# Attention of a two-layer hybrid decoder on one core: four heads a step in row quarters, rotary on another engine, keys ahead of values

## The chip, the cores and the metric

One core of a Trainium2 chip runs the whole program: two layers of a decoder for one sequence of 256 positions, in float32. The metric is the device time of one execution in microseconds. Engines are named as the profile names them: PE is TensorE (PEld its weight loads), DVE is VectorE, ACT is ScalarE, POOL is GpSimd, SP is SyncE, whose queue issues all DMAs here.

## The reference, cut to what matters

Each layer projects the normed input with one matrix, whose columns belong to a gated DeltaNet branch (16 heads of 128), a sliding-window attention branch (32 query heads of 64, 4 key/value heads, window 128) and two output gates:

```python
h   = rmsnorm(x, norm_w) * (1.0 + scale) + shift      # adaLN: shift, scale, gate from c
u   = h @ w_in
qkv_a, beta_a, a_a, z_a, q_b, k_b, v_b, z_b, g_a, g_b = split_cols(u, SPLIT_SIZES)
qkv_a = silu(causal_conv(qkv_a, conv_w))              # then l2norm of q_a and k_a per head
beta, g = sigmoid(beta_a), -exp(a_log) * softplus(a_a + dt_bias)
o_a = rmsnorm(gated_delta_rule(q_a, k_a, v_a, g, beta), gdn_norm_w) * silu(z_a)
q_b, k_b = rope(q_b, positions), rope(k_b, positions) # [x1 cos - x2 sin, x2 cos + x1 sin], halves of 32
o_b = swa_with_sinks(q_b, k_b, v_b, sinks) * silu(z_b)
y   = sigmoid(g_a) * (o_a @ proj_a) + sigmoid(g_b) * (o_b @ proj_b)
x   = x + gate * (y @ w_out)
```

The delta rule works in chunks: it forms decayed Gram products of the keys, solves a unit lower triangular system, and passes one state per head on. Attention scores have a causal window of 128, a learned sink logit per head in the softmax's denominator, and two blocks of 128 queries, the second of which sees the first block's keys too.

## The kernel before, in words

Activations lie transposed, channels on partitions and the 256 positions along the free dimension. The unit of work is one projection: a tile of 128 output columns of a weight matrix, contracted over 16 blocks of 128 channels. Weights come in halves of 128x1024 by DMA (`load_half`, lines 198 to 205); ACT rounds each to a high part (`whi`, L203) and DVE subtracts to get the low part (`wlo`, L204), so that float32 accuracy comes from matmuls in the rounded type: 16 of 512 columns with the high weights (L291) and 16 of 256 with the low ones (L292). There are five buffers for a loaded half, four for the high and three for the low part, and two PSUM banks (`psm`) for projections. `evac` (L317 to L320) takes a projection out of PSUM: ACT copies one half, DVE adds the other (L319). So the projection after next needs DVE's sum.

`_plan` (L46) lists a layer's projections in order; the gates of layer 0 and eight of layer 1 are done ahead in other code. Then follow `ba` (decay and beta), `kb` and `vb` (attention keys and values of two key/value heads each), and for each of two batches of eight DeltaNet heads: eight queries `qa`, eight values `va`, eight keys `ka`, and eight pairs of `qb` and `zb` (attention queries and their gate, two heads each). In the second batch the second `kb` and `vb` stand between values and keys. After both batches come `za` (the DeltaNet gate), and the three output matrices `pa`, `pb`, `wo`.

Each projection has a handler (`h_qa`, `h_zb`, ...), which runs as the code is written out. A handler may be a generator: `yield n` puts what follows behind n further projections beside the next one (`streams`, `advance`). One further generator per batch, `gdn`, is the delta rule; `run_bg(1)` writes out one of its steps after each projection. It is appended when the batch's last pair of keys has been handled. Its parts: decay and key norms (`E`, `GT`, L603, L615), Gram products (L623 to L626), a triangular solve of 32-row blocks as a chain of 62 DVE operations (L643 to L651), block products on PE (L673 to L705), and `gdn_core` with the state and the outputs. `ADA_RATE` says how many conditioning jobs (`ada_job`: two DMAs of 512 KB and two DVE operations, L170) go with each projection.

What is written out is not the order in which an engine works. The tile layer orders each engine's instructions ahead of time: an instruction written earlier goes first, unless by the layer's own durations its operands are not there yet; then later ones pass it. In the trace the product of L634, written late in `gdn_k`, runs in the value stage. On the chip each engine keeps that order and waits where an operand comes later.

An attention pair: `rope` (L793) shifts 32-row quarters with four DMAs and makes three POOL operations (L798, L799, L801); the scores (L836) contract the 64 rows of one head, the two heads of a pair in the two halves of the array's rows; DVE reduces them (L843, L845), ACT takes exponentials and scales, PE transposes (L864), ACT copies, PE multiplies by the values (L872, L873), DVE multiplies by the gate, and a DMA stores. Small PSUM tiles come from a ring of six banks (`psg`).

## Time and profile before

| what | value |
| --- | --- |
| median of 3 runs | 2387.16 us (2384.02 to 2390.58) |
| profiled execution | 2388.38 us, span 2386.6 us, granted TensorE clock 0.991 |
| PE busy | 2306.3 us, 97% |
| PEld busy | 2024.4 us, 85% |
| DVE busy | 1793.7 us, 75% |
| ACT busy | 1426.7 us, 60% |
| POOL busy | 120.3 us, 5% |
| DMA | 222 GB/s of HBM traffic over the span |
| chain that ended last | PE 70%, DVE 14%, DMA 9%, issue 3%, ACT 3%, POOL 1% |

The span is the time from the first to the last instruction. Busy time is the union of an engine's instructions; matmuls are pipelined, so a busy PE is not PE at its peak, and an idle PE is a real loss. The chain is followed back from the last instruction, at each step to what released it. By the order of projections in the trace, layer 0 has its DeltaNet and attention stages from 218 to 942 us and layer 1 from 1273 to 1968 us; layer 0 also carries most of the conditioning jobs.

### The profile page before, as it was taken

To read this page: it belongs to the slowest core of one execution; us is meant where nothing else is said; L and a number is where in the kernel's file an instruction comes from. 1 tells how busy PE (TensorE), PEld (TensorE's weight loads), DVE (VectorE), ACT (ScalarE), POOL (GpSimd) and SP (SyncE) were. 2 spreads that over 40 slices of the span, in tenths; PEclk is the share of its full clock that TensorE was granted. 3 is DMA by queue.
4 is the path that set the end of the run, shared out by engine and by line. 5 is a ranking of instruction groups with operands and counts; after the bars stand their busy time and mean duration, and the time that the engine had idled before them with its cause. 6 is when DMAs were issued, how large, how long until landed. Compare 5 with 4: busy or idle time off the path is not lost.

```text
span 2386.6 us, 40186 instructions
## 1 busy us (share of the span) xinstructions
PE 2306.3 (97%) x14838; PEld 2024.4 (85%) x14838; DVE 1793.7 (75%) x3117; ACT 1426.7 (60%) x2676; POOL 120.3 (5%) x128
## 2 busy tenths in 40 slices
PE   7999999999999999999999999999999999999997
PEld 6999787878878888888888888888888888888886
DVE  7998878877787868888676777856678457677766
ACT  4436656777657755444455667777677665444442
POOL 0000000120002100000000001100011000000000
PEclk9999999999999999999999999999999999999999
DMA  9998667566776567998756555555555557777764
GB/s 364 361 360 280 227 223 246 157 192 200 229 234 196 175 220 263 329 308 304 226 191 205 177 179 171 163 181 163 190 170 163 172 179 269 241 247 245 245 202 144
DMA packets 192519, 536.50 MB, mean 225 GB/s; under 512 B 42753, under 2 KB 76609, under 8 KB 186817
## 3 DMA queue, kind: packets, MB, share of 16 engines
q1 hardware_dynamic: 192322, 533.93, 67.1%
q8 instruction: 117, 1.92, 0.3%
q14 instruction: 80, 0.66, 0.1%
HBM read 512.26 MB, written 16.88 MB: 222 GB/s over the span
## 4 chain that ended last, share of the span: by engine, by line
PE 70%; DVE 14%; DMA 9%; issue 3%; ACT 3%; POOL 1%; SPq 0%; DVEq 0%; ACTq 0%; POOLq 0%
PE mm L291 35%; PE mm L292 18%; DVE wlo L204 5%; DMA adaw<-ada 3%; PE mmg L253 2%; PE mmg L251 2%; PE mmg L252 2%; DMA win<-w 2%; DMA xs_dram<-x 1%; DVE LX L649 1%; DMA rr<-rr_d 1%; DVE mt L647 1%; DVE cv L526 1%; ACT whi L203 1%; PE sc L836 1%
## 5 line engine op out<-in xcount | busy, mean ns | idle before, releaser
L291 PE MATMUL mm<-h,whi 128*128 128x512 f32 x3616 | 1298.0, 399 | 15.3 <-DVE ub L319 15.0
L204 DVE TENSOR_TENSOR wlo<-win,whi 128x1024 fp32r<-128x1024 f32 x724 | 886.2, 1227 | 302.6 <-PE mm L292 181.2
L292 PE MATMUL mm<-h,wlo 128*128 128x256 f32 x3616 | 1028.9, 285 | 0.0
L203 ACT CAST whi<-win 128x1024 fp32r<-128x1024 f32 x724 | 755.0, 1048 | 418.5 <-PE mm L291 237.7
L291 PEld LDWEIGHTS mm<-h,whi 128*128 128x128 f32 x3616 | 684.1, 189 | 172.4 <-issue 8.7
L292 PEld LDWEIGHTS mm<-h,wlo 128*128 128x128 f32 x3616 | 684.9, 189 | 1.4 <-issue 0.6
L170 DVE SCALAR_TENSOR_TENSOR adaw<-adaw,cact 128x1024 f32<-128x1024 f32 x128 | 156.0, 1225 | 58.6 <-DMA adaw<-ada 58.4
L291 PE MATMUL mm<-yhl,whi 128*128 128x512 f32 x512 | 181.1, 396 | 5.0 <-DVE x L926 3.4
L291 PE MATMUL mm<-oAhl,whi 128*128 128x512 f32 x512 | 180.8, 395 | 0.3 <-ACT whi L203 0.3
L291 PE MATMUL mm<-oBhl,whi 128*128 128x512 f32 x512 | 180.7, 396 | 0.0
L319 DVE TENSOR_TENSOR ub<-ub,mm 128x256 f32<-128x256 f32 x290 | 120.5, 415 | 60.5 <-ACT ub L318 60.4
L526 DVE SCALAR_TENSOR_TENSOR cv<-ub,par,cv 128x253 f32<-128x253 f32 (+2 forms) x288 | 137.7, 480 | 34.8 <-ACT cv L524 31.0
L292 PE MATMUL mm<-oAhl,wlo 128*128 128x256 f32 x512 | 144.3, 282 | 1.4 <-DVE wlo L204 1.4
L251 PE MATMUL mmg<-h,whi 128*128 128x256 f32 x512 | 139.5, 287 | 6.3 <-ACT h L376 6.1
L292 PE MATMUL mm<-yhl,wlo 128*128 128x256 f32 x512 | 144.4, 282 | 0.0
L292 PE MATMUL mm<-oBhl,wlo 128*128 128x256 f32 x512 | 144.1, 281 | 0.0
L252 PE MATMUL mmg<-h,whi 128*128 128x256 f32 x512 | 142.5, 286 | 0.1
L253 PE MATMUL mmg<-h,wlo 128*128 128x256 f32 x512 | 135.5, 287 | 3.2 <-DVE wlo L204 3.2
L318 ACT COPY ub<-mm 128x256 f32<-128x256 f32 x290 | 106.7, 368 | 47.0 <-PE mm L292 45.0
L291 PEld LDWEIGHTS mm<-yhl,whi 128*128 128x128 f32 x512 | 96.2, 188 | 29.5 <-issue 5.5
L291 PEld LDWEIGHTS mm<-oAhl,whi 128*128 128x128 f32 x512 | 96.1, 188 | 23.2 <-ACT whi L203 0.6
L291 PEld LDWEIGHTS mm<-oBhl,whi 128*128 128x128 f32 x512 | 96.2, 188 | 22.9
(260 smaller groups left out, 2764.3 us busy)
## 6 DMA issues: line engine op xcount, KB each, us to landing
win<-w SPq DMA_DIRECT2D x724, 512.0 KB, 4.9
adaw<-ada SPq DMA_DIRECT2D x128, 512.0 KB, 5.0
adab<-ada SPq DMA_DIRECT2D x31, 1024.0 KB, 8.9
sg<-sig_dram SPq DMA_DIRECT2D x40, 128.0 KB, 3.0
rot<-ub SPq DMA_DIRECT2D x144, 32.0 KB, 3.0
sig_dram<-gacc SPq DMA_DIRECT2D x4, 1024.0 KB
E<-gc_dram SPq DMA_DIRECT2D x4, 1024.0 KB
GT<-GT_d SPq DMA_DIRECT2D x4, 1024.0 KB
```

What stands on the lines that cost most here:

```text
L170: V.scalar_tensor_tensor(t, t, 1.0, cact[:, hf * 1024:(hf + 1) * 1024], op0=ALU.mult, op1=ALU.mult, accum_out=acc[:, hf:hf + 1])
L203: A.copy(h, w)
L204: V.tensor_tensor(o, w, h.bitcast(F32), op=ALU.subtract)
L251: T.matmul(d, hi, m[:, 0:S], start=(k == b0 and t % 2 == 0), stop=False)
L252: T.matmul(d, hi, m[:, S:2 * S], start=False, stop=False)
L253: T.matmul(d, lo, m[:, 0:S], start=False, stop=(k == b1 - 1 and t % 2 == 1))
L291: T.matmul(ps[:, :], hi[k // 8][:, c0:c0 + P], m, start=(k == 0), stop=False)
L292: T.matmul(ps[:, S:2 * S], lo[k // 8][:, c0:c0 + P], m[:, 0:S], start=False, stop=(k == KT - 1))
L318: A.copy(t, ps[:, S:2 * S])
L319: V.tensor_tensor(t, t, ps[:, 0:S], op=ALU.add)
L526: V.scalar_tensor_tensor(y[:, j:], u[:, :S - j], w(3 - j), y[:, j:], op0=ALU.mult, op1=ALU.add)
L647: V.tensor_tensor(tv, Xt[:, 0:j + 1, j:j + 1].broadcast_to([64, j + 1, n]), Lt[:, j:j + 1, j + 1:32].broadcast_to([64, j + 1, n]), op=ALU. ...
```

## The change

The plan puts both `kb` and both `vb` first, keys ahead of values in each batch, and attention as eight steps of four projections per layer: two of queries, two of gates. A query tile now holds one rotary half (32 channels) of four heads, one head of each key/value group, in the four 32-row quarters; the next tile holds the other halves. Key tiles are packed in the same way. Rotary then needs no shift: six DVE operations on whole tiles (`rope`), where four DMAs and three POOL operations stood for each tile. The sign column of the sine table goes.

A step (`h_zb`, every second gate) has four heads: scores as two accumulated products of 32 rows in one row quarter per head, four score banks; the softmax over four heads at once; transposes three projections later instead of two, copied back in place; values one projection after that, for two gate tiles; then both stores. The score matmuls are written right behind the second gate's projection.

The decay chain of `h_ba` is cut in three by yields. Pair transposes of `qa`, `ka` and `va` (`sumsq`, L723) are written after two further projections instead of one. One more background step stands before the block products of the solve. The conditioning rate of value projections falls from 0.35 to 0, that of attention projections rises from 0.1 to 0.275, in layer 0. The value tile of attention gets two buffers, `zbs` and the table scratch four.

```diff
-ADA_RATE = [dict(qa=0.45, ka=0.45, va=0.35, qb=0.1, zb=0.1, za=0.54, pa=0.54, pb=0.54), dict(ga=0.3, pa=0.3, gb=0.3, pb=0.3)]
+ADA_RATE = [dict(qa=0.45, ka=0.45, va=0.0, qb=0.275, zb=0.275, za=0.54, pa=0.54, pb=0.54), dict(ga=0.3, pa=0.3, gb=0.3, pb=0.3)]
...
-    p += [("ba", 0), ("kb", 0), ("vb", 0)]
+    p += [("ba", 0), ("kb", 0), ("kb", 1), ("vb", 0), ("vb", 1)]
     for b in range(NB):
-        for what in ("qa", "va", "ka"):
+        for what in ("qa", "ka", "va"):
             p += [(what, b * HB + h) for h in range(HB)]
-            if b == 1 and what == "va":
-                p += [("kb", 1), ("vb", 1)]
-        for t in range(8 * b, 8 * b + 8):
-            p += [("qb", t), ("zb", t)]
+        for j in range(4 * b, 4 * b + 4):
+            p += [("qb", 2 * j), ("qb", 2 * j + 1), ("zb", j), ("zb", 8 + j)]
...
-    if what == "qb":
-        return OFF_QB + _pair_rows(i)
+    if what in ("qb", "kb"):
+        heads = (i // 2 + 8 * np.arange(4)) if what == "qb" else np.arange(4)
+        return {"qb": OFF_QB, "kb": OFF_KB}[what] + (64 * heads[:, None] + 32 * (i % 2) + np.arange(32)).reshape(-1)
...
+            sink4 = sm.tile([P, 8, 4, 2], F32, name="sink4", tag="sink4", bufs=1)
...
             def h_ba(ps, i):
                 u = evac(ps)
+                yield 0
...
                 V.tensor_tensor(q, q, na.unsqueeze(1).broadcast_to([P, 2, NH]), op=ALU.mult)
+                yield 1
                 pg = gps("gcp", [P, 3, NH])
...
                 A.activation(egc1, gc[:, 1, :], AF.Exp)
+                yield 0
                 s = cols_to_rows(gc.rearrange("p m h -> p (m h)"), 2 * NH, "gcr")
...
                 conv_silu(ps, i, g["qT"][:, hh, :])
                 if hh % 2 == 1:
-                    yield 0
+                    yield 1
                     sumsq(g["qT"], g["ssq"], hh - 1)
...
                 conv_silu(ps, 16 + i, g["kT"][:, hh, :])
                 if hh % 2 == 1:
-                    yield 0
+                    yield 1
                     sumsq(g["kT"], g["ssk"], hh - 1, g["kdec"])
...
                         dma(d, xdr[:, blk].rearrange("q j i -> j q i"))
                 yield 1
                 yield 1
+                yield 1
                 GTv = GT.rearrange("p h m t -> p (h m) t")
...
                 pair = (g["vT"], vT)
-                yield 0
+                yield 1
                 p = gps("vtr", [P, 2, 2, P])
...
-            def rope(u, dst_pairs):
-                rot = sm.tile([P, S], F32, name="rot", tag="tB", bufs=2)
-                for a in range(4):
-                    c = a ^ 1
-                    dma(rot[32 * a:32 * a + 32, :], u[32 * c:32 * c + 32, :])
-                G.tensor_tensor(rot, rot, stab, op=ALU.mult)
-                G.tensor_tensor(u, u, ctab, op=ALU.mult)
-                for rows, dst in dst_pairs:
-                    G.tensor_tensor(dst, u[rows], rot[rows], op=ALU.add)
+            def rope(lo, hi, dst):
+                a = sm.tile([P, S], F32, name="rot", tag="tB", bufs=2)
+                V.tensor_tensor(a, hi, stab, op=ALU.mult)
+                b = sm.tile([P, S], F32, name="rot", tag="tB", bufs=2)
+                V.tensor_tensor(b, lo, stab, op=ALU.mult)
+                V.tensor_tensor(lo, lo, ctab, op=ALU.mult)
+                V.tensor_tensor(dst[:, 0, :], lo, a, op=ALU.subtract)
+                V.tensor_tensor(hi, hi, ctab, op=ALU.mult)
+                V.tensor_tensor(dst[:, 1, :], hi, b, op=ALU.add)
+
+            def halves(ps, i, name):
+                u = evac(ps)
+                if i % 2 == 0:
+                    st["lo"] = u
+                    return
+                r = sm.tile([P, 2, S], F32, name=name, tag=name, bufs=1)
+                rope(st["lo"], u, r)
+                st[name] = r
 
             def h_kb(ps, i):
-                u = evac(ps)
-                kp = sm.tile([P, S], F32, name="kr", tag="kr", bufs=1)
-                rope(u, [(slice(0, 128), kp)])
-                kpad[i] = kp
+                halves(ps, i, "kr")
...
-                v = sm.tile([P, 2, P], F32, name="vnat", tag="vnat", bufs=1)
+                v = sm.tile([P, 2, P], F32, name="vnat", tag="vnat", bufs=2)
...
-            def h_qb(ps, t):
-                u = evac(ps)
-                q = sm.tile([P, S], F32, name="qr", tag="tC", bufs=1)
-                rope(u, [(slice(0, 128), q)])
-                st["q"] = q
+            def h_qb(ps, i):
+                halves(ps, i, "qr")
 
             def h_zb(ps, t):
                 z = evac(ps)
-                zs = sm.tile([P, S], F32, name="zbs", tag="tD", bufs=3)
+                zs = sm.tile([P, S], F32, name="zbs", tag="tD", bufs=4)
                 A.activation(zs, z, AF.Silu)
-                q = st["q"]
-                yield 0
-                j = t // 8
-                kp, vn = kpad[j], vnat[j]
-                sc = [gps("sc", [P, 3 * P]) for _ in range(2)]
-                for e, m in ((0, 0), (1, 1), (0, 1), (1, 0)):
-                    r = slice(64 * e, 64 * e + 64)
-                    T.matmul(sc[e][:, m * P:(2 * m + 1) * P], q[r, m * P:(m + 1) * P], kp[r, 0:(m + 1) * P],
-                             start=True, stop=True)
-                pb = sm.tile([P, 2, 3 * P], F32, name="pb", tag="pb", bufs=1)
-                nm = sm.tile([P, 2, 2], F32, name="nm", tag="nm")
-                ls = sm.tile([P, 2, 2], F32, name="ls", tag="ls")
-                for e in range(2):
-                    ns = nsink[:, 2 * t + e:2 * t + e + 1]
+                if t < 8:
+                    st["z"] = zs
+                    return
+                j = t - 8
+                gates = (st["z"], zs)
+                q, k = st["qr"], st["kr"]
+                sc = [gps("sc", [P, 3 * P]) for _ in range(4)]
+                for m in range(2):
+                    for c in range(2):
+                        for e in range(4):
+                            r = slice(32 * e, 32 * e + 32)
+                            T.matmul(sc[e][:, m * P:(2 * m + 1) * P], q[r, c, m * P:(m + 1) * P],
+                                     k[r, c, 0:(m + 1) * P], start=(c == 0), stop=(c == 1))
+                pb = sm.tile([P, 4, 3 * P], F32, name="pb", tag="pb", bufs=1)
+                nm = sm.tile([P, 4, 2], F32, name="nm", tag="nm")
+                ls = sm.tile([P, 4, 2], F32, name="ls", tag="ls")
+                for e in range(4):
+                    ns = nsink[:, 4 * j + e:4 * j + e + 1]
                     V.tensor_tensor_reduce(pb[:, e, 0:P], sc[e][:, 0:P], amask[:, P:2 * P], -0.125, ns,
                                            ALU.add, ALU.min, nm[:, e, 0:1])
                     V.tensor_tensor_reduce(pb[:, e, P:3 * P], sc[e][:, P:3 * P], amask, -0.125, ns,
                                            ALU.add, ALU.min, nm[:, e, 1:2])
-                for e in range(2):
+                for e in range(4):
                     A.activation(pb[:, e, 0:P], pb[:, e, 0:P], AF.Exp, bias=nm[:, e, 0:1], scale=-1.0,
                                  accum_out=ls[:, e, 0:1])
                     A.activation(pb[:, e, P:3 * P], pb[:, e, P:3 * P], AF.Exp, bias=nm[:, e, 1:2], scale=-1.0,
                                  accum_out=ls[:, e, 1:2])
-                V.tensor_tensor(nm, nm, sink4[:, t], op=ALU.add)
+                V.tensor_tensor(nm, nm, sink4[:, j], op=ALU.add)
                 A.activation(nm, nm, AF.Exp)
                 V.tensor_tensor(ls, ls, nm, op=ALU.add)
                 V.reciprocal(ls, ls)
-                for e in range(2):
+                for e in range(4):
                     A.mul(pb[:, e, 0:P], pb[:, e, 0:P], ls[:, e, 0:1])
                     A.mul(pb[:, e, P:3 * P], pb[:, e, P:3 * P], ls[:, e, 1:2])
-                yield 1
+                yield 2
                 ptS = []
-                for e in range(2):
+                for e in range(4):
                     pt = gps("ptr", [P, 3, P])
                     for c in range(3):
                         T.transpose(pt[:, c, :], pb[:, e, c * P:(c + 1) * P], ident)
-                    ps_ = sm.tile([P, 3, P], F32, name="pts", tag="pts")
-                    A.copy(ps_, pt)
-                    ptS.append(ps_)
-                yield 1
-                po = gps("pv", [P, S])
-                for e in (1, 0):
-                    r = slice(64 * e, 64 * e + 64)
-                    T.matmul(po[r, :], vn[:, 0, r], ptS[e][:, 0:2, :], start=True, stop=False)
-                    T.matmul(po[r, P:S], vn[:, 1, r], ptS[e][:, 2, :], start=False, stop=True)
-                V.tensor_tensor(zs, zs, po, op=ALU.mult)
-                dma(ob_dram[t], zs)
+                    p = pb[:, e, :].rearrange("p (c q) -> p c q", c=3)
+                    A.copy(p, pt)
+                    ptS.append(p)
+                yield 0
+                for f in range(2):
+                    po = gps("pv", [P, S])
+                    vn = vnat[f]
+                    for e in (1, 0):
+                        r = slice(64 * e, 64 * e + 64)
+                        p = ptS[2 * f + e]
+                        T.matmul(po[r, :], vn[:, 0, r], p[:, 0:2, :], start=True, stop=False)
+                        T.matmul(po[r, P:S], vn[:, 1, r], p[:, 2, :], start=False, stop=True)
+                    V.tensor_tensor(gates[f], gates[f], po, op=ALU.mult)
+                    dma(ob_dram[8 * f + j], gates[f])
```

The rest moves the sink logits into the new order of heads.

## Rows read from the trace of the kernel before

**Rows 1.** Stretches: start:end, length; busy us of PE, PEld, DVE, ACT, POOL; clock; DMA.

```profile
2103.40:2283.20 179.80, 179.80 (x1026) 157.21 (x1025) 128.60 (x186) 86.73 (x127) 0.00 (x0) 1.00 0.73 240
291.10:342.40 51.30, 47.63 (x275) 40.95 (x274) 41.22 (x66) 29.65 (x61) 0.00 (x0) 1.00 0.70 235
```

**Rows 2.** PE's waits: who waited for whom: us in total, times, longest us.

```profile
PE mm L291 <- DVE ub L319: 15.0, 12, 2.6
PE sst L533 <- ACT kT L527: 8.5, 7, 3.0
PE vtr L723 <- ACT vT L527: 7.7, 6, 1.9
...
PE sc L836 <- POOL qr L801: 3.5, 4, 1.3
...
PE gcp L502 <- DVE spq L500: 3.2, 2, 1.8
```

**Rows 3.** Stretches: one attention pair, then the four that hold a solve.

```profile
446.14:460.04 13.90, 13.90 (x87) 11.68 (x87) 10.78 (x32) 11.52 (x25) 2.20 (x3) 1.00 0.59 190
...
447.00:493.00 46.00, 43.28 (x259) 36.20 (x258) 41.36 (x103) 34.55 (x72) 8.16 (x9) 0.96 0.61 195
765.00:805.00 40.00, 38.50 (x241) 32.22 (x240) 39.07 (x103) 29.30 (x59) 6.27 (x6) 1.00 0.53 169
1480.00:1534.00 54.00, 52.87 (x336) 44.53 (x335) 46.64 (x113) 39.46 (x78) 12.59 (x14) 1.00 0.52 164
1779.00:1832.00 53.00, 51.77 (x327) 43.50 (x327) 46.58 (x113) 38.48 (x78) 11.43 (x13) 1.00 0.53 161
```

**Rows 4.** PE in order of time, end of one pair: start us, us, instruction, count.

```profile
458.43 0.66 PE L872 MATMUL pv<-pts,vnat 128*64 128x256 f32 x4
...
459.24 0.87 PE L864 MATMUL ptr<-cst,pb 128*128 128x128 f32 x6
460.04 0.93 PE L836 MATMUL sc<-kr,qr 64*128 64x128 f32 x8
460.89 0.50 PE L291 MATMUL mm<-h,whi 128*128 128x512 f32 x1
```

**Rows 5.** PE groups by shape, first attention stage: count, busy us, mean ns, idle before.

```profile
L836 PE MATMUL sc<-kr,qr 64*128 64x256 f32 x32 | 7.2, 402 | 0.0
L836 PE MATMUL sc<-kr,qr 64*128 64x128 f32 x32 | 6.9, 297 | 2.5 <-POOL qr L801 2.5
```

**Rows 6.** DVE groups: whole kernel (first), layer 1's first attention stage (others).

```profile
L170 DVE SCALAR_TENSOR_TENSOR adaw<-adaw,cact 128x1024 f32<-128x1024 f32 x128 | 156.0, 1225 | 58.6 <-DMA adaw<-ada 58.4
...
L319 DVE TENSOR_TENSOR ub<-ub,mm 128x256 f32<-128x256 f32 x16 | 6.6, 411 | 4.1 <-ACT ub L318 4.1
L845 DVE CUSTOM_DVE_ANT_0 pb<-sc,cst,nsink 128x256 f32<-128x256 f32 x12 | 5.7, 475 | 0.0
L843 DVE CUSTOM_DVE_ANT_0 pb<-sc,cst,nsink 128x128 f32<-128x128 f32 x12 | 4.1, 342 | 1.8 <-PE sc L836 1.8
```

**Rows 7.** One line's and one tile's instructions: count: ns min/median/max, first and last start.

```profile
L204 DVE TENSOR_TENSOR wlo<-win,whi x724: 1161/1222/1809, 17.9 to 2365.3; 128x1024 fp32r<-128x1024 f32 x181
...
L647 DVE TENSOR_TENSOR mt<-LX x124: 183/368/958, 452.1 to 1837.0; 64x31 f32<-64x31 f32 x8, 64x60 f32<-64x60 f32 x8, 64x87 f32<-64x87 f32 x8, 64x112 f32<-64x112 f32 x8
L649 DVE TENSOR_TENSOR LX<-LX,mt x124: 182/357/976, 452.4 to 1837.2; 64x31 f32<-64x31 f32 x8, 64x60 f32<-64x60 f32 x8, 64x87 f32<-64x87 f32 x8, 64x112 f32<-64x112 f32 x8
```

**Rows 8.** DVE in order of time; POOL rotates from 466.86 to 469.56.

```profile
451.25 0.16 DVE L852 TENSOR_TENSOR nm<-nm,sink 128x4 f32<-128x4 f32 x1
...
465.63 0.39 DVE L649 TENSOR_TENSOR LX<-LX,mt 64x231 f32<-64x231 f32 x1
...
467.08 0.70 DVE L852 TENSOR_TENSOR nm<-nm,sink 128x4 f32<-128x4 f32 x1
...
468.13 0.83 DVE L649 TENSOR_TENSOR LX<-LX,mt 64x240 f32<-64x240 f32 x1
468.89 0.69 DVE L854 TENSOR_TENSOR ls<-ls,nm 128x4 f32<-128x4 f32 x1
```

More of the change, by code (lines that the diff above doesn't have):

```diff
@@ L87, in _tile_cols @@
         return c
-    if what == "qb":
-        return OFF_QB + _pair_rows(i)
+    if what in ("qb", "kb"):
+        heads = (i // 2 + 8 * np.arange(4)) if what == "qb" else np.arange(4)
+        return {"qb": OFF_QB, "kb": OFF_KB}[what] + (64 * heads[:, None] + 32 * (i % 2) + np.arange(32)).reshape(-1)
     if what == "zb":
         return OFF_ZB + _pair_rows(i)
-    off = {"ka": OFF_K, "va": OFF_V, "qa": OFF_Q, "kb": OFF_KB, "vb": OFF_VB,
+    off = {"ka": OFF_K, "va": OFF_V, "qa": OFF_Q, "vb": OFF_VB,
            "za": OFF_ZA, "ga": OFF_GA, "gb": OFF_GB}[what]
@@ L99 @@
 CC_ID, CC_TRI, CC_DM, CC_AM, CC_IF = 0, 128, 256, 384, 640
-NCC = 642
+NCC = 641
 def _consts():
@@ L115, in _consts @@
     c[:, CC_IF] = inv[i % half]
-    c[:, CC_IF + 1] = np.where((i % 64) < half, -1.0, 1.0)
     return c
@@ L338, in rope_tables @@
                 n = sm.tile([P, S], F32, name="nrot", tag="tC", bufs=1)
-                r = sm.tile([P, S], F32, name="rred", tag="tD", bufs=3)
+                r = sm.tile([P, S], F32, name="rred", tag="tD", bufs=4)
                 V.tensor_scalar(n, ang, 1.0 / (2.0 * math.pi), shift, op0=ALU.mult, op1=ALU.add)
@@ L441, in build @@
             edec = sm.tile([P, NH], F32, name="edec", tag="edec")
-            sink4 = sm.tile([P, 16, 2, 2], F32, name="sink4", tag="sink4", bufs=1)
-            V.tensor_copy(sink4, pr[:, PC_SINK:PC_SINK + 32].rearrange("p (t e) -> p t e", e=2).unsqueeze(3)
-                          .broadcast_to([P, 16, 2, 2]))
+            sink4 = sm.tile([P, 8, 4, 2], F32, name="sink4", tag="sink4", bufs=1)
+            V.tensor_copy(sink4, pr[:, PC_SINK:PC_SINK + 32].rearrange("p (t e) -> p t e", e=4).unsqueeze(3)
+                          .broadcast_to([P, 8, 4, 2]))
             nsink = sm.tile([P, 32], F32, name="nsink", tag="nsink", bufs=1)
@@ L449, in build @@
             yA = [None, None]
-            kpad, vnat = [None, None], [None, None]
+            vnat = [None, None]
             sig = {}
@@ L1051, in pack @@
     par = np.zeros((L, P, NPC), np.float32)
-    heads = np.concatenate([_pair_heads(t) for t in range(16)])
+    heads = np.concatenate([j + 8 * np.arange(4) for j in range(8)])
     for l in range(L):
```

1 line of the change is left out of this document (removed).

## The prediction

> **What bounds the kernel now.** I read the busy shares first, then the stages as stretches, then TensorE's own waits, then one attention pair instruction by instruction, and last VectorE. Where nothing else happens, 32 projections take 179.80 us, 5.62 us each, with TensorE busy throughout at a granted clock of 1.00 [rows 1]. That is the floor: a change can gain only what TensorE does or waits for between projections. The reader is to see that in the layer-0 value stage of the first batch the same eight projections, with their pair transposes, leave TensorE idle for 51.30 - 47.63 = 3.7 us [rows 1], and that the waits name the causes: transposes that wait for ScalarE's SiLU output (keys 8.5 us in 7 waits, values 7.7 us in 6), score matmuls that wait for GpSimd's rotary add (3.5 us in 4), and projections that wait for VectorE to empty a PSUM bank (15.0 us in 12) [rows 2].
>
> One undisturbed attention pair is 13.90 us from score block to score block [rows 3], so beside two projections (11.24) it costs 2.66. Its blocks start at 458.43 (values), 459.24 (transposes), 460.04 (scores), and the projections go on at 460.89 [rows 4]: 0.81, 0.80 and 0.85 us, and 0.2 more in the first projection matmul, which is longer than usual (0.50). What is work in it? The 256-column score matmul is 105 ns longer than the 128-column one (402 against 297) [rows 5], so 128 columns are 0.105 us. Per head a pair streams four score records of 128, 128, 256 and 256 columns, 768 in all, 0.63 us; both heads of the pair run at once, since eight records fit into 0.85 us. The value block has as many columns, 0.63. Six transposes are 6 x 0.105 = 0.63. So 1.89 us is work and 0.77 is four changes of the array's shape (projection to values, to transposes, to scores, to projection), 0.19 each.
>
> VectorE is the second limit. The triangular solve of the delta rule is a chain of 62 operations, and in the four stretches that hold it TensorE is idle by 46.00 - 43.28, 40.00 - 38.50, 54.00 - 52.87 and 53.00 - 51.77, together 6.6 us [rows 3].
>
> **The change, part by part.**
>
> *Later transposes.* Pair transposes of queries, keys and values are written one projection later than now, 5.6 us. The longest of the waits is 3.0 us for keys and 1.9 for values [rows 2], so the operand is there before its new place. Gain 8.5 + 7.7 = 16.2 us. What is late next is the square sums, which nobody needs for several projections. Bounds: 0 (if the order on the engines doesn't follow) to 16.2. I take all of it.
>
> *Rotary on VectorE.* Thirty-six rotations, each of four small copies in SyncE's queue and three GpSimd operations, become 18 of six VectorE operations. The scores were waiting for these; now two projections lie between the rotation and its scores. Gain 3.5 us [rows 2]. 144 DMA issues leave SyncE's queue; no TensorE wait of weight that I saw hangs on it, so nothing is taken for them.
>
> *Row quarters.* A step has four heads. Its scores contract 32 rows twice where a pair contracted 64 once: 2 x 768 columns per head, 1.26 us if the four quarters run at once. Values are 2 x 0.63, twelve transposes 1.26, and there are three changes of shape (projection to values to scores to projection; the transposes now stand between projections of their own shape): 3 x 0.19. Sum 4.35 against 2 x 2.66 = 5.32, 0.97 us for each of 16 steps, 15.5. I take 13, since some of the transposes' 0.80 may be a start that stays. The trace before shows only two row tiles at once, so the bounds come from it: four at once 1.26 us; two at once 2.52, which costs 20 us over all steps; one at a time 5.04, which costs 60. I take four, because the two that are shown do not delay each other at all: eight records with 1.26 us of columns take 0.85.
>
> The Trainium skill's "TensorE: Matmul & The Clock Gate" (Measured speedup vs the span model) gives 3.07 times for four row tiles, not 4. By it the scores of a step would be 5.04 / 3.07 = 1.64 us, an estimate, and the forecast 0.38 x 16 = 6 us higher, about 2374.
>
> *The solve under a heavier VectorE.* Keys ahead of values starts the delta rule's background work six projections earlier against the attention stage: its decay and Gram products fall into the value stage, and the solve into the first attention step instead of the second pair onward. I count six projections that hold the solve. Fixed VectorE work per projection is two splits of 1.22 and one PSUM sum of 0.41 [rows 6, 7]: 2.85, so 17.1. The solve is 31 x (0.368 + 0.357) = 22.5 [rows 7].
> Before: three pairs' score reductions, each 2 x (0.342 + 0.475) = 1.63 [rows 6], 4.9; three value products of 0.41, 1.2; three small softmax groups of about 0.47, 1.4; and three times what GpSimd takes away: with a rotation running, operations that take 0.16 and 0.39 us otherwise took 0.70, 0.83 and 0.69 [rows 8], 1.5 us for each rotation, 4.5. Sum 51.6 us against TensorE's 3 x 13.90 = 41.7: 9.9 too much. TensorE lost 1.1 and 1.2 us there in layer 1 [rows 3], so some 8.7 us are absorbed by split weights and PSUM banks held ready.
> After: two rotations of 6 x 0.41 = 4.9, one step's reductions 3.3, softmax 0.5, nothing for GpSimd. Sum 17.1 + 22.5 + 4.9 + 3.3 + 0.5 = 48.3 us. TensorE has less beside it, because the first step has no values yet: 6 x 5.62 + 1.7 for scores + 1.3 for transposes = 36.7. Too much by 11.6; less 8.7 leaves 2.9 us idle. In layer 0 the conditioning rate in these projections rises from 0.1 to 0.275 jobs, with two operations of 1.225 [rows 6] and small ones, 2.6 us a job: 6 x 0.275 x 2.6 = 4.3 more, 7.2 idle. Both layers and batches: 2 x (2.9 + 7.2) = 20.2, instead of 6.6: a cost of 13.6 us. Bounds: a gain of 6.6 if all is absorbed, a cost of 55.0 - 6.6 = 48.4 if nothing is. The queue behind a late solve is the PSUM sum of the last projection; the projection after next waits for it.
>
> The Trainium skill's "SBUF — State Buffer" (SBUF: two separate sides) says that a GpSimd operation that reads SBUF and a VectorE operation with two SBUF inputs exclude each other for the whole instruction. By it a rotation would hold VectorE for all three of its operations, some 0.75 us each by the undisturbed ones, 2.2 and not 1.5: the absorbed amount would be 2.2 us larger in each of four phases, and the forecast some 9 us lower, about 2359. The 0.16 us operation that took 0.70 agrees in kind.
>
> *At nothing.* The decay chain in three parts: its matmul waits 3.2 us in two layers [rows 2]; it is placed where its input is expected, and that does not move with where it is written, so 0, with 3.2 either way. Second keys and values projected early: the same two projections. Fewer ScalarE table loads: ScalarE does not end TensorE's waits there. One more background step before the block products: they already wait for no DMA. The conditioning rate of value projections going to 0 is repaid in the attention stage, counted above.
>
> **Sum.** -16.2 - 3.5 - 13.0 + 13.6 = -19.1. The profiled execution took 2388.4 us; 2369.3 follows, and as it lies 1.2 above the median of the runs, 2368.
>
> **The rivals.**
> - *VectorE absorbs it all.* The planner fills VectorE's free time in the value stage, where layer 0 now has no conditioning (VectorE 41.22 of 51.30 before [rows 1]), and the solve is hidden: 2388.4 - 32.7 - 6.6 - 1.2 = 2348. Against it: that stage now takes in the Gram products.
> - *VectorE absorbs nothing (slower).* With the value stage full, no split weights are held ready when the solve starts, and every too-much is idle TensorE: +48.4, 2388.4 - 32.7 + 48.4 - 1.2 = 2403. It decides from where less than (55.0 - 6.6 - 32.7) / 4 = 3.9 us per solve is absorbed. For it: solves already show in TensorE's idle time; against it: 8.7 is absorbed now.
> - *Quarters run two at a time.* +20: 2388, no change. For it: the trace shows no more than two.
> - *The transposes' waits stay.* If the planner still puts them where it believes the operand ready, the change does not do what it says there: +16.2, 2384. Against it: written later, they rank behind a whole further projection.
>
> **How the numbers follow.** Forecast 0.42, all absorbed 0.20, nothing absorbed 0.15, two at a time 0.11, waits stay 0.12. A measurement of this kernel can tell about 0.3% (7 us) from no change. Faster, below 2380: most of the forecast (0.36), all absorbed (0.20) and a little of waits stay: 0.60. Slower, above 2394: most of nothing absorbed and a rest of the two others: 0.18. Within: 0.22. The likeliest case by itself reaches from 2355 to 2381; the range takes in both VectorE rivals in most of their extent: 2344 to 2400.
>
> **What would show it.** Right: no wait of a pair transpose for SiLU above a few tenths; score records of four heads starting within hundredths of each other and a step's block near 1.7 us; GpSimd without rotations; TensorE's waits for the PSUM sum rising above 15.0 us, bunched at the solves and larger in layer 0. Wrong: scores near 3 us a step; the value stages longer than the 47 us they need; a new wait for PSUM banks, since a step takes four of six at once.

## The result, and the profile after

The changed kernel takes 2376.31 us (median of 13 runs, 2370.66 to 2384.38) where the kernel before, run beside it, takes 2388.88 (13 runs): ratio 0.9947, 95% interval 0.9937 to 0.9957. That is 12.6 us faster; the forecast was 2368, 8 us too low. The profiled execution took 2373.67 us, span 2371.9, 14.7 less than the span before.

The page after, busy time of each engine:

```profile
PE 2294.8 (97%) x15094; PEld 2026.0 (85%) x15094; DVE 1791.0 (76%) x3176; ACT 1372.8 (58%) x2621; POOL 13.9 (1%) x20
```

TensorE's busy time was 2306.3, so it fell by 11.5; its idle time fell only from 80.3 to 77.1. GpSimd is nearly empty (13.9 us, 120.3 before).

TensorE's waits after; columns as in [rows 2]:

```profile
PE mm L289 <- DVE ub L317: 19.4, 16, 3.1
...
PE mm L290 <- DVE wlo L202: 4.9, 5, 2.2
PE mm L289 <- DVE x L937: 4.6, 5, 1.7
PE mm L289 <- DVE oAhl L322: 3.3, 1, 3.3
...
PE sst L533 <- ACT qT L527: 1.4, 2, 1.2
PE T1p L679 <- DMA mt<-xdr: 1.3, 1, 1.3
```

Against [rows 2], four waits are gone: keys 8.5, values 7.7, rotated queries 3.5, decay sum 3.2, together 22.9. Since idle time fell by 3.2 only, 19.7 of other waiting has come, most of it for VectorE: 15.0 has become 19.4 for the PSUM sum (L317), 1.4 has become 4.9 for split weights in projections (L202), and the split of the DeltaNet output (L322) is new.

The end of one four-head attention step on TensorE, in order of time; it answers to [rows 4]:

```profile
1782.06 0.66 PE L883 MATMUL pv<-pb,vnat 128*64 128x256 f32 x4
...
1783.56 1.59 PE L844 MATMUL sc<-kr,qr 32*128 32x128 f32 x32
1785.08 0.50 PE L289 MATMUL mm<-h,whi 128*128 128x512 f32 x1
```

Values take 1.50 us (1782.06 to 1783.56) and scores 1.52; the twelve transposes, elsewhere in the step, 1.31 by the ends of their records. Together 4.33. The whole step is more, since the first matmul of the projection that goes on is longer (0.50, otherwise 0.39). From score block to score block, the measure of [rows 3], with TensorE busy throughout and no other work on it:

```profile
1756.40:1783.56 27.16, 27.16 (x189) 23.29 (x189) 26.78 (x77) 21.84 (x47) 0.00 (x0) 1.00 0.49 158
```

27.16 us, less four projections of 5.62, leaves 4.68 for a step. Two pairs took 27.80, so a step saves 0.64 us.

Where the time went, by the first matmul of each stage in the two profiled executions (us):

| stretch | before | after | difference |
|---|---|---|---|
| ahead of layer 0's projections | 218.1 | 216.4 | -1.7 |
| layer 0, through the gates of the delta rule | 723.4 | 713.5 | -9.9 |
| layer 0, the output matrices and what follows | 331.8 | 346.3 | +14.5 |
| layer 1, through the gates | 694.9 | 677.5 | -17.4 |
| layer 1, the rest | 418.3 | 418.1 | -0.2 |

The third line was in no forecast: layer 0 gives back 14.5 us where the change edits nothing. TensorE is idle there for 17.5 us, before for 10.0, and the granted clock is lower (0.97 in the first of the three matrices, where it was 1.00).

Last, the solves. Stretches from the first to the last of the 62 operations of each, two of layer 1 and two of layer 0 (columns as in [rows 1]):

```profile
1462.25:1503.64 41.39, 41.39 (x266) 35.78 (x266) 40.30 (x113) 27.55 (x57) 0.00 (x0) 1.00 0.47 156
1741.05:1782.44 41.39, 41.39 (x266) 35.78 (x266) 40.30 (x113) 27.55 (x57) 0.00 (x0) 1.00 0.51 165
409.24:460.10 50.86, 47.70 (x313) 40.55 (x312) 47.91 (x127) 29.53 (x60) 0.00 (x0) 0.93 0.57 185
705.51:753.58 48.07, 46.51 (x318) 39.18 (x318) 45.77 (x126) 28.71 (x59) 0.00 (x0) 1.00 0.62 204
```

In layer 1 TensorE is busy in all of both stretches, although VectorE is busy for 40.30 of 41.39 us. In layer 0 the same solve takes 6.7 to 9.5 us longer, and TensorE loses 3.16 and 1.56.

### The profile page after: what moved, and what is told of

Read it like the earlier page. It is cut to its first block, busy times and chain, and to the rows that moved or that the text cites. A ratio compares the mean times of both kernels' runs of the same rounds, so it can differ in the third digit from the quotient of the medians.

```text
span 2371.9 us, 40130 instructions
## 1 busy us (share of the span) xinstructions
PE 2294.8 (97%) x15094; PEld 2026.0 (85%) x15094; DVE 1791.0 (76%) x3176; ACT 1372.8 (58%) x2621; POOL 13.9 (1%) x20
## 4 chain that ended last, share of the span: by engine, by line
PE 76%; DVE 11%; DMA 8%; issue 3%; ACT 2%; DVEq 0%; SPq 0%; ACTq 0%
PE mm L289 39%; PE mm L290 20%; DVE wlo L202 4%; DMA adaw<-ada 4%; PE mmg L251 2%; PE mmg L250 2%; PE mmg L249 2%; DMA win<-w 2%; DMA xs_dram<-x 1%; DVE adaw L168 1%; PE o L742 1%; PE ptr L872 1%; DVE cv L526 1%; PE sc L844 1%; PE mmg L273 1%
## 5 line engine op out<-in xcount | busy, mean ns | idle before, releaser
L202 DVE TENSOR_TENSOR wlo<-win,whi 128x1024 fp32r<-128x1024 f32 x724 | 882.5, 1221 | 253.0 <-PE mm L290 142.8
L168 DVE SCALAR_TENSOR_TENSOR adaw<-adaw,cact 128x1024 f32<-128x1024 f32 x128 | 155.9, 1222 | 71.4 <-DMA adaw<-ada 70.1
L317 DVE TENSOR_TENSOR ub<-ub,mm 128x256 f32<-128x256 f32 x290 | 120.8, 417 | 63.8 <-ACT ub L316 62.7
L526 DVE SCALAR_TENSOR_TENSOR cv<-ub,par,cv 128x255 f32<-128x255 f32 (+2 forms) x288 | 138.2, 480 | 34.1 <-ACT cv L524 30.4
```

The source lines that it names most:

```text
L168: V.scalar_tensor_tensor(t, t, 1.0, cact[:, hf * 1024:(hf + 1) * 1024], op0=ALU.mult, op1=ALU.mult, accum_out=acc[:, hf:hf + 1])
L202: V.tensor_tensor(o, w, h.bitcast(F32), op=ALU.subtract)
L317: V.tensor_tensor(t, t, ps[:, 0:S], op=ALU.add)
L526: V.scalar_tensor_tensor(y[:, j:], u[:, :S - j], w(3 - j), y[:, j:], op0=ALU.mult, op1=ALU.add)
```

## The experiments

Ratios are to the kernel before, timed beside each, with 95% intervals; the changed kernel's own is 0.9947.

### Are the later transposes worth 16 us, and alone?

*a_soon*: the changed kernel with its pair transposes back at the next projection.

```
 # queries, keys, values
-yield 1
+yield 0
```

> The changed kernel with one part undone: the pair transposes of queries, keys and values are written one projection after their inputs again, not two. Theory (the later transposes removed waits that were a loss of their own): the waits of transposes for ScalarE return, some 14 us in layer 0 and 1 to 2 in layer 1, against 1.4 us in the changed kernel: about 2390 us, near the kernel before. Rival (VectorE is simply late in layer 0, and a wait that is lifted at a transpose shows up at the next PSUM sum): 2376 to 2381, the waits change their name and the idle time stays.

Measured 2389.94 us, 1.0018 (1.0003 to 1.0032): the whole gain is gone, 14 us by the medians and 17 by the ratios. Waits for queries (3.9) and keys (6.0) are back.

*b_late*: the kernel before with the same edit the other way (`yield 0` to `yield 1`, the three places).

> The kernel before with this one part alone: pair transposes of queries, keys and values written one projection later. Theory: 15 us fewer, about 2374, as good as the whole change; transposes wait for less than 2 us in all. Rival (lateness only moves on): 2383 to 2389, with TensorE's waits for the PSUM sum rising from 15 us by about as much.

Measured 2400.84 us, 1.0050 (1.0026 to 1.0074): slower, which neither theory had. Its waits:

```profile
PE mm L291 <- DVE ub L319: 21.6, 17, 3.1
PE sc L836 <- POOL qr L801: 16.7, 7, 4.6
PE T1p L678 <- DMA mt<-xdr: 7.1, 3, 3.2
```

The waits for keys and values went as they should, but the last key transpose is what starts the delta rule, so its work moved with them (the four solves begin 7 to 20 us later), and met others: rotated queries 16.7 instead of 3.5, the solve's own transfer 7.1 instead of nothing. One such meeting is seen in SyncE's queue and on GpSimd (start us, us, instruction, count), in b_late and then in the kernel before:

```profile
1760.35 0.51 SPq L797 DMA_DIRECT2D rot<-ub  x1
1760.97 0.53 SPq L467 DMA_DIRECT2D GT<-GT_d  x1
1761.55 2.71 SPq L797 DMA_DIRECT2D rot<-ub  x3
1769.23 1.14 POOL L798 TENSOR_TENSOR rot<-rot,stab 128x256 f32<-128x256 f32 x1 [15.64 <-DMA rot<-ub]
1770.33 1.70 POOL L799 TENSOR_TENSOR ub<-ub,ctab 128x256 f32<-128x256 f32 x1
1772.11 1.58 POOL L801 TENSOR_TENSOR qr<-ub,rot 128x256 f32<-128x256 f32 x1
```

```profile
1761.09 2.42 SPq L797 DMA_DIRECT2D rot<-ub  x4
1764.82 0.74 POOL L798 TENSOR_TENSOR rot<-rot,stab 128x256 f32<-128x256 f32 x1 [11.57 <-DMA rot<-ub]
1765.52 0.74 POOL L799 TENSOR_TENSOR ub<-ub,ctab 128x256 f32<-128x256 f32 x1
1766.34 1.60 POOL L801 TENSOR_TENSOR qr<-ub,rot 128x256 f32<-128x256 f32 x1
```

In b_late a transfer of the delta rule (GT, part of its decay) is issued between the four small copies of a rotation, and GpSimd begins that rotation at 1769.23; in the kernel before the rotation nearest to it has its four copies issued together at 1761.09 and begins at 1764.82. The rotation's operations are also longer in b_late, 4.4 us together against 3.1. How much each of the two adds to the wait was not tried.

*b_late3*: b_late with two more delays, to take these two collisions away and nothing else.

```
 # h_zb, ahead of the scores (rotated queries in two buffers)
-yield 0
+yield 1
 # gdn_k, ahead of T1: a third pause, as in the changed kernel
+yield 1
```

> The kernel before with the transposes one projection later as in b_late, and two more delays: the scores one projection later, and the third pause in the solve that the changed kernel has. Theory (the later transposes alone were slower because they moved the solve onto the rotary swaps and its own round trip: 16.7 us of waits of the scores on GpSimd's rotated queries and 7.1 us on the solve's transfer, against 3.5 and none before): both waits go, with some of the half-speed stretches behind them, so 2400.8 - 16.7 - 7.1 - 3 to 8 = 2369 to 2374 us. Rival (they only come out elsewhere, on VectorE): 2385 to 2400 us.

Measured 2369.05 us, 0.9928 (0.9915 to 0.9941), 16.4 us faster than its kernel before (2385.49). Neither collision is among its waits, and the 3.5 us for rotated queries that the kernel before has are gone too, so up to 3.5 of the gain can be theirs. The later transposes are worth 13 to 16 us, near what they were forecast at, but only with the delta rule and the rotation kept apart. The change has both (a third pause, and a rotation without copies), which the forecast had booked at nothing and at 3.5.

### What eats the rest: conditioning, and the order of keys and values

*a_noada* and *b_noada*: the changed kernel and the one before with the conditioning products on 8 of 1024 columns; the transfers stay, and the conditioning is left out of the result.

```
-V.scalar_tensor_tensor(t, t, 1.0, cact[:, hf * 1024:(hf + 1) * 1024], ...)
+V.scalar_tensor_tensor(t[:, 0:8], t[:, 0:8], 1.0, cact[:, hf * 1024:hf * 1024 + 8], ...)
```

> The changed kernel with the conditioning products of the projection loop left out but for 8 of 1024 columns (the DMAs stay), so VectorE has 128 x 1.15 = 147 us less work, nearly all of it in layer 0. Theory (what layer 0 gives back is VectorE's crowding by conditioning): layer 0's DeltaNet, attention and output stages lose their idle time, some 35 us: 2340. Against the kernel before with the same products left out it gains 25 us or more, as layer 1 does in each layer (17). Rival (the give-back comes from the conditioning's DMAs or from the order of work): 2365 to 2376, and the lead over the other stays near 13.

> The kernel before with the same conditioning products left out. Theory: its layer 0 becomes like its layer 1, whose DeltaNet and attention stages are 28 us shorter: 2355 to 2365, 20 to 35 above the changed kernel without them. Rival (order or DMAs): 2375 to 2388, 13 above the changed kernel without them.

Measured 2339.98 us, 0.9800 (0.9779 to 0.9822), and 2371.06, 0.9942 (0.9920 to 0.9964). By these ratios the products cost the kernel before 0.58% of its time, 14 us (17 by the medians), and the changed one 0.9947 - 0.9800 = 1.47%, 35 us. Without them the change is worth 1.42%, 34 us (31 by the medians). The theory for a_noada came true in its number; the kernel before gained less than its theory said.

*a_oldrate*: the old rates of conditioning per projection.

```
-va=0.0, qb=0.275, zb=0.275
+va=0.35, qb=0.1, zb=0.1
```

> The changed kernel with the old conditioning rates of layer 0 (0.35 for values, 0.1 for attention projections). Theory (VectorE in layer 0 is short wherever background work and conditioning meet): the value stage, which now holds the Gram products, gets 2.8 jobs of 2.6 us per batch, and the attention stages lose as many; the idle time of 10 and 9 us that the two attention stages of layer 0 hold falls by 4 to 6 each and the value stages lengthen by 2 to 6 each: 2372 to 2380. Rival (the solve alone makes the idle time, conditioning has no part): attention stages unchanged, 2376 within 3.

Measured 2371.01 us, 0.9928 (0.9911 to 0.9944). That is 4.5 us below the changed kernel by the ratios, and the intervals overlap: if the rates matter by themselves, it is by little.

*a_oldorder*: values ahead of keys, as before.

```
-for what in ("qa", "ka", "va"):
+for what in ("qa", "va", "ka"):
```

> The changed kernel with values ahead of keys again in each batch, so that decay, Gram products and solve start seven projections later, in the attention stage. Theory (the earlier start moves TensorE's background work out of the DeltaNet gate's stage, where VectorE then has too little time beside it in layer 0, and puts the solve beside attention's first step): layer 1 the same within 3 us; in layer 0 the gate's and output stages get back 5 to 10 us and the attention stages hold the solve beside conditioning at 0.275 as before: 2366 to 2376. Rival (the early start is what pays in layer 1): layer 1 loses 5 or more, 2380 to 2386.

Measured 2360.70 us, 0.9884 (0.9867 to 0.9901): 15 us faster than the changed kernel, and below both forecasts. The rates go with the names, so this also moved conditioning from the second stage of a batch to the third. *a_kazero* moves that alone and keeps the new order.

```
-ka=0.45, va=0.0
+ka=0.0, va=0.45
```

> The changed kernel, keys ahead in both layers, with layer 0's conditioning taken from the key projections (0.45 to 0) and given to the value projections (0 to 0.45): the rate that the old order has beside the decay tables is set without the old order. Theory (the order lost because it set 0.45 products per projection beside the 16 table operations at the start of each batch: the key stages took 50.8 and 48.5 us here, 46.6 without such products): 2363 to 2370 us. Rival (it is the order: the state recurrence now beside the scores, with conditioning there too): within 4 us of the changed kernel, 2372 to 2380 us.

Measured 2368.13 us, 0.9929 (0.9912 to 0.9946). Its key stages are clean: the stage of the first batch in the changed kernel, then in this one:

```profile
295.40:346.20 50.80, 48.37 (x275) 42.26 (x272) 41.39 (x69) 30.07 (x76) 0.00 (x0) 0.97 0.74 244
```

```profile
297.40:344.10 46.70, 46.70 (x276) 41.15 (x274) 35.87 (x54) 30.09 (x76) 0.00 (x0) 1.00 0.61 196
```

So the theory's number came out (2363 to 2370), but not its reason: beside the kernel before the total gains only some 4 us on the changed kernel (0.9929 against 0.9947), with intervals that overlap. Between a_kazero and a_oldorder conditioning stands in the same stage and the order alone differs: 0.9929 against 0.9884, about 11 us, with intervals apart. So the order is most of the 15.

*a_mixorder*: values ahead of keys in layer 0 alone.

```
-for what in ("qa", "ka", "va"):
+for what in (("qa", "va", "ka"), ("qa", "ka", "va"))[l]:
```

> The changed kernel with values ahead of keys in layer 0 only; layer 1 keeps keys ahead. Theory (the order costs where conditioning shares VectorE, and pays where it doesn't): by the two profiles, layer 0 ended at 1257.8 us with values ahead and at 1276.2 with keys ahead, and what followed took 1101.1 us with values ahead and 1095.7 with keys ahead, so the mixture's span is 1257.8 + 1095.7 = 2353.5 and its time 2355 us. Rival (the 5.4 us in layer 1 are stalls that fall anew with every edit): 2360 to 2363 us, as with values ahead in both layers.

Measured 2357.26 us, 0.9887 (0.9870 to 0.9903), which can't be told from a_oldorder. The profiles agree with the theory in layer 1 (1095.4 us against 1101.1), but the medians don't settle 3 us. It and a_oldorder are the fastest versions that leave nothing out.

*a_mix_noada*: a_mixorder with the products shrunk as in a_noada.

> As a_mixorder (values ahead of keys in layer 0 alone), with layer 0's conditioning products on 8 of 1024 columns, as in a_noada; the conditioning is left out of the result. Theory (the order costs only by what shares VectorE with it in layer 0; without the conditioning both orders end that layer together, at 1245 us): 2335 to 2342 us, as a_noada's 2339.98. Rival (the state recurrence beside the scores costs by itself, conditioning or not): the 19 us that values ahead saved in layer 0 stay, 2319 to 2326 us. In between, the share that stays is the order's own.

Measured 2347.87 us, 0.9834 (0.9813 to 0.9854): no faster than a_noada with keys ahead (0.9800), rather slower. The rival falls, and the theory fell short: without conditioning the new order in layer 0 is no cost, and perhaps a gain of 8 us. With values ahead the products cost 0.9887 - 0.9834 = 0.53%, 13 us, as in the kernel before; with keys ahead, 35. The order and the conditioning cost together, not each by itself; by what mechanism the order matters beside the products stays open.

How a product delays TensorE shows in the changed kernel's VectorE at the start of its longest key-stage wait (start us, us, instruction, idle before):

```profile
297.19 1.22 DVE L202 TENSOR_TENSOR wlo<-win,whi 128x1024 fp32r<-128x1024 f32 x1
300.81 1.23 DVE L168 SCALAR_TENSOR_TENSOR adaw<-adaw,cact 128x1024 f32<-128x1024 f32 x1 [2.40 <-DMA adaw<-ada]
...
301.96 1.22 DVE L202 TENSOR_TENSOR wlo<-win,whi 128x1024 fp32r<-128x1024 f32 x1
303.10 0.41 DVE L317 TENSOR_TENSOR ub<-ub,mm 128x256 f32<-128x256 f32 x1
```

The product stands first in VectorE's queue and its weights have not landed: VectorE, the crowded engine, does nothing for 2.40 us, and the PSUM sum that TensorE needs (L317) comes behind it, after the product and a split; TensorE waits 2.4. Over the run VectorE lost 70.1 us to this line in 52 waits, before 58.4 [rows 6]. No run took this wait away while it kept the products. a_noada kept it and took the products; VectorE's wait in layer 0 (216 to 1280 us), in the changed kernel and then in a_noada:

```profile
DVE adaw L168 <- DMA adaw<-ada: 47.1, 30, 3.3
```

```profile
DVE adaw L168 <- DMA adaw<-ada: 51.3, 38, 4.0
```

VectorE waits as long for these transfers, yet TensorE's idle time falls from 77.1 to 55.2 us over the run. So the wait alone does not make the loss; it costs where the products' own time comes on top of it.

### Two prices

*a_ropeG*: the six rotary operations on GpSimd instead of VectorE.

```
-V.tensor_tensor(a, hi, stab, op=ALU.mult)   # and the five others
+G.tensor_tensor(a, hi, stab, op=ALU.mult)
```

> The changed kernel with its six rotary operations on GpSimd, which is idle, instead of VectorE. Theory (GpSimd holds VectorE up while it rotates: 0.54, 0.44 and 0.54 us were lost in one rotation of three operations): VectorE loses about 3 us for each of 18 rotations of six and saves 2.1 to 2.5: no gain, 2374 to 2384. Rival (any work taken off VectorE pays in layer 0): 2366 to 2372.

Measured 2388.92 us, 1.0010 (0.9997 to 1.0024): 12.6 us worse than the changed kernel, the gain gone, and above the theory's 2384. The solve on VectorE, layer 1's first batch, in a_ropeG and then in the changed kernel (31 pairs of operations; count, busy us, mean ns, idle before):

```profile
L649 DVE TENSOR_TENSOR LX<-LX,mt 64x31 f32<-64x31 f32 (+15 forms) x31 | 13.1, 423 | 0.6
L647 DVE TENSOR_TENSOR mt<-LX 64x31 f32<-64x31 f32 (+15 forms) x31 | 12.9, 417 | 0.7
```

```profile
L647 DVE TENSOR_TENSOR mt<-LX 64x31 f32<-64x31 f32 (+15 forms) x31 | 10.3, 331 | 0.4
L649 DVE TENSOR_TENSOR LX<-LX,mt 64x31 f32<-64x31 f32 (+15 forms) x31 | 10.2, 330 | 0.3
```

26.0 against 20.5 us: VectorE does 4.9 us less of rotary work in a solve's stretch (two rotations of 6 x 0.41) and spends 5.5 more on the solve's own operations. That is close to the theory's price, 3 us lost for each rotation; what it left out are the waits that come back, 6.4 us for the decay sum and 3.7 for rotated queries, and TensorE's idle time in the solves' stretches, 12.7 us in all where the changed kernel has 4.7.

The Trainium skill's "SBUF — State Buffer" (SBUF: two separate sides) says that a GpSimd operation that reads SBUF and a VectorE operation with two SBUF inputs shut each other out for the whole instruction. These are such operations, and the trace agrees in kind: both sides are longer. GpSimd's two operations that write the result took 786 and 892 ns in the median for queries, and 744 and 738 for keys, which are rotated ahead of the delta rule.

*a_onebank*: each weight block as three matmuls of 256 columns that add up in one PSUM half, so that VectorE has no PSUM sum left to make.

```
-T.matmul(ps[:, :], hi, m, ...)             # 512 columns
-T.matmul(ps[:, S:2 * S], lo, m[:, 0:S], ...)
+T.matmul(ps, hi, m[:, 0:S], ...)
+T.matmul(ps, hi, m[:, S:2 * S], ...)
+T.matmul(ps, lo, m[:, 0:S], ...)
```

> The changed kernel with all three products of a projection added up in the same 256 columns of PSUM (three matmuls of 256 columns for each block instead of one of 512 and one of 256, the high weights loaded twice), so that VectorE's sum at the end of a projection goes: 290 x 0.41 = 119 us less on VectorE, a third more weight loads. Theory (VectorE's lateness is the remaining idle time of TensorE in layer 0): idle time falls by 15 to 25 us, 2352 to 2362, if a third matmul keeps the 0.118 us for 256 columns that the gate stage's matmuls of this form take. Rival (TensorE pays for the third weight load, 5 ns or more for each of 5152 blocks): 2385 and above, although VectorE waits less.

Measured 2400.26 us, 1.0054 (1.0035 to 1.0072), as the rival had it. VectorE got 116 us lighter (1675.2 busy), yet TensorE's wait moved to the operation beside it, the split of the weights:

```profile
PE mm L291 <- DVE wlo L202: 22.4, 17, 2.8
```

The third weight load has a price too. The stretch of 32 projections without other work, which took 179.80 us [rows 1], here:

```profile
2116.90:2298.90 182.00, 182.00 (x1539) 182.00 (x1538) 116.96 (x154) 88.61 (x127) 0.00 (x0) 1.00 0.73 238
```

1.2% longer, with weight loads busy throughout (157.21 us before). Over all 322 projections that is some 20 us, so the run is no clean measure of what VectorE's sum costs.

## Why the prediction was right, and where not

**Later transposes (-16.2): right in size, incomplete in cause.** Keys and values wait no more, 1.0 more is waited for queries. a_soon gives 14 to 17 us, b_late3 13 to 16. "What is late next is the square sums, which nobody needs" missed that the last of them starts the delta rule; b_late paid for that.

**Rotary wait (-3.5): right**, and too low for what the step does: in a_ropeG the six operations on GpSimd cost 12.6, without any copies.

**Row quarters (-13): right in mechanism, too high in size.** A step saves 0.64 us and not 0.97, so 16 steps save 10.2. The three blocks take what was worked out (4.33 us, 4.35 in the sum); the sum left out what a block adds to the projection matmuls around it, some 0.35 us a step, while the 2.66 for a pair, taken from score block to score block, had it in. Scores take 1.52 us, with a change of shape in it; without one of 0.19, 1.33 for 1.26 of columns. The four quarters do run at once: the first records of the four heads start at 1783.56, 1783.57, 1783.57 and 1783.58. The 1.64 estimated from the Trainium skill's "TensorE: Matmul & The Clock Gate" (Measured speedup vs the span model) is too long for this case.

**Decay chain (0): wrong by 3.2**, a gain: its wait is gone. In layer 0 its matmul starts 28.2 us after the first projection, before 24.9. Two things can have put it later, the cut into three parts and the second keys and values ahead of it; they were not tried apart.

**VectorE at the solves (+13.6): this step failed, on both sides.** In layer 1 it forecast 2.9 us idle a batch, and in the solves' stretches there is none. The mis-sized term is VectorE's need, "48.3 us" a solve as a sum of durations. The 111 instructions that lie wholly in the first stretch of layer 1 add up to 46.7 us indeed, but VectorE is busy for 40.30, since each operation begins about 0.07 us before the one ahead of it ends (start us, us, instruction):

```profile
1469.70 1.21 DVE L202 TENSOR_TENSOR wlo<-win,whi 128x1024 fp32r<-128x1024 f32 x1
1470.84 0.34 DVE L649 TENSOR_TENSOR LX<-LX,mt 64x192 f32<-64x192 f32 x1
1471.10 0.41 DVE L798 TENSOR_TENSOR rot<-ub,stab 128x256 f32<-128x256 f32 x1
```

The "8.7 absorbed" in the kernel before was mostly this overlap, taken for slack: in its first solve of layer 1 the durations add up to 48.9 us, and VectorE is busy for 43.15 of 44.26 (columns as in [rows 1]):

```profile
1495.16:1539.42 44.26, 43.08 (x267) 36.02 (x266) 43.15 (x115) 32.99 (x69) 8.48 (x9) 1.00 0.54 180
```

The time beside it was too short as well: the solve lies across seven projections, 41.39 us of TensorE's work, and not six with 36.7. Need and time nearly balance, and nothing waits. In layer 0 four products come on top: 47.91 busy of 50.86.

There the forecast counted 7.2 a batch, and 4.4 and 5.3 came at the two solves (3.1 and 1.5 in the stretches above, the rest right behind them: start us, us, instruction, idle before):

```profile
468.17 0.22 PE L679 MATMUL T1p<-mt,GT 32*32 32x32 f32 x2 [1.32 <-DMA mt<-xdr]
```

```profile
760.50 0.38 PE L290 MATMUL mm<-h,wlo 128*128 128x256 f32 x1 [2.20 <-DVE wlo L202]
762.74 0.28 PE L679 MATMUL T1p<-mt,GT 32*32 32x32 f32 x2 [1.61 <-issue]
```

So TensorE's idle time at the solves went from 6.6 [rows 3] to 9.7 us: +3.1 where +13.6 was forecast. The sign that the waits for the PSUM sum would bunch at the solves did not come: in the four attention stages they are 6.0 us, before 6.6; the rise to 19.4 lies elsewhere in layer 0. That the value stages exceed 47 us (55.3 and 55.1 in layer 0) told nothing, since the Gram products lie in them now: in layer 1 they take 53.9 without idle time.

What the forecast left out is everything else in layer 0: conditioning that meets the tables in the key stages (a_kazero), and the end of the layer, 14.5 us longer. Of these, 7.5 are idle time of TensorE and 5.8 half speed, as worked out below. In one profiled execution of each, the end takes 336.0 us without the products (a_noada; 331.8 before, 346.3 after) and 338.3 and 340.7 with values ahead of keys (a_oldorder, a_mixorder). In these two the gates' stage ahead of it is as long as before (119.7 and 119.4 us, before 123.3), where the changed kernel has 102.8: there work that stood in that stage now lies in the attention. In a_kazero, with a gates' stage of 103.7, the end takes 343.4. So it hangs on the products and on the order; that VectorE comes out of a shorter gates' stage with less in hand would fit, but was not tried by itself.

**A term that was missing: half speed.** Behind several of these waits TensorE's clock is found lower. Stretches of 4 us around and after the ends of the waits at 303.66 (2.4 us) and 441.05 (3.1 us) in the changed kernel; the clock is the third number from the end:

```profile
300.00:304.00 4.00, 1.57 (x9) 1.14 (x8) 3.19 (x5) 0.80 (x3) 0.00 (x0) 0.98 0.59 176
304.00:308.00 4.00, 4.00 (x16) 3.38 (x15) 3.56 (x8) 2.13 (x5) 0.00 (x0) 0.59 0.90 279
440.00:444.00 4.00, 2.95 (x9) 2.59 (x10) 3.85 (x11) 3.10 (x9) 0.00 (x0) 0.55 0.80 253
444.00:448.00 4.00, 4.00 (x15) 3.42 (x15) 2.85 (x5) 1.55 (x3) 0.00 (x0) 0.60 0.44 155
```

A granted clock of 0.59 over 4 us is a mixture of full speed (2.4 GHz) and half (1.2). What it costs is read from matmuls at either level (start us, us, instruction):

```profile
304.26 0.63 PE L289 MATMUL mm<-h,whi 128*128 128x512 f32 x1
...
304.90 0.63 PE L289 MATMUL mm<-h,whi 128*128 128x512 f32 x1
...
307.73 0.40 PE L289 MATMUL mm<-h,whi 128*128 128x512 f32 x1
...
308.09 0.39 PE L289 MATMUL mm<-h,whi 128*128 128x512 f32 x1
```

From one matmul with the high weights to the next, with one of the low weights between, it is 0.64 us at half speed and 0.36 at full, so some 0.45 of TensorE's busy time in such a stretch is lost: 1.5 us behind the first wait and 2.8 behind the second, beside the waits themselves. Summed over such stretches from 60 us on, without the kernel's end, that is 10.7 us before, 14.1 after, and 18.7 in b_late. It counts as busy time.

In one sum: forecast -16.2 - 3.5 - 13.0 + 13.6 = -19.1. Measured in the span: waits gone -22.9, packing -10.2, other waits +19.7, half speed +3.4, remainder -4.7, together -14.7. The remainder was not tried; it would fit that other work on TensorE cuts into projections at 138 places after and 162 before, 24 fewer, which at 0.19 us each (an estimate, the prediction's price of a change of shape) is 4.6.

That the total came within 8 us is in part luck. The solves cost 10.5 us less in idle time than forecast and the decay wait's 3.2 went unforecast, while packing saved 2.8 less and the end of layer 0, in no term, took 14.5: errors larger than the one of the total, which nearly cancel. Of the rivals, two at a time and staying waits are excluded; VectorE absorbs the solves in layer 1 and not in layer 0.

## What to carry to other kernels

Read an engine's need in a stage from its busy time in a stretch, not from a sum of durations, since neighbours overlap. A delay that is free where it is made can move what hangs on it into a collision elsewhere, so the same edit can be worth some -15 us in one schedule and +13 in another. Background work on the crowded engine cost 13 us in one order here and 35 in the other; try the order and the background together, and price a wait with the half-speed stretch that may follow. Compare two versions of a block by one measure: from block to block, or by the block's own records, not one against the other.

## What the runs showed of the hardware

- Four 32-row score matmuls run side by side at 1.33 us for 1.26 us of columns.
- In projections of three matmuls of 256 columns for a block, each with a weight load, the weight loads were busy throughout (182.00 of 182.00 us) and a projection took 5.69 us; with 512 and 256 columns and two loads, 157.21 of 179.80 us and 5.62.
- VectorE's small operations start about 0.07 us before the end of the one ahead. In a stretch with two rotations on GpSimd beside them the solve's operations were 26 to 28% longer in the mean (331 to 417 ns and 330 to 423).
- Waits of 2.4 and 3.1 us on TensorE were followed by stretches at half the clock that cost 1.5 and 2.8 us more.
